# A list scheduler's durations for matmuls and transposes, replaced in a 22,915-instruction kernel

## The chip, the cores and the metric

The kernel runs on one core of one Trainium2 chip. The metric is device time in microseconds (us) of one execution, the median of the runs taken.

## The reference

Two transformer blocks in a row on 256 tokens of width 1024, float32 throughout, each followed by a norm:

```
memn = rmsnorm(mem)
layer 0: x += ab_mixer(rmsnorm(x));  x += cross_attn(rmsnorm(x), memn);  x += relu(h @ w1)^2 @ w2
layer 1: x += c_mixer(rmsnorm(x));   x += cross_attn(rmsnorm(x), memn);  x += relu(h @ w1)^2 @ w2
second block, layer 0: h += pool_mixer(rms_norm(h));     h += conv_glu_ffn(rms_norm(h))
second block, layer 1: h += window_attn(rms_norm(h));    h += conv_glu_ffn(rms_norm(h))
out = rms_norm(h)
```

`ab_mixer` is half a gated linear attention, half stick-breaking attention; `c_mixer` is a gated delta rule (short convolutions, a triangular inverse for each of 8 heads, then a chain of products for each head). The window attention has 16 heads. The weights are 1 MB blocks of float32, each used once.

## The kernel before, in words

**Arithmetic.** A float32 matrix is split on the chip into a high part (`hi`, ScalarE, line 402, a cast to the type float32r) and the rest (`lo`, VectorE, line 406). `mm3` (line 521) then issues three float32r matmuls, hi x hi, hi x lo, lo x hi, into one PSUM bank. This is nearly all the work: matmuls with 256 moving columns (`lin_b`, line 576) or with 512 (`second`, line 657, which adds a stage's result to the residual `xs`). Plain float32 matmuls, which appear as two instructions each, do the small products of the mixers; transposes (`tr`) are matmuls against an identity (`base` in the trace).

**Staging.** Each weight block goes by DMA to one of 2 `raw` buffers, is split into one of 3 `hi` and 3 `lo` buffers, and is consumed by 24 or 48 matmuls. The 8 PSUM banks (`pb`), 9 scratch tiles, 10 large tiles and 4 hidden pairs are slots that operations compete for.

**The order of instructions.** Nothing runs as it is written. Each helper calls `plan.add(engine, cost, ...)`, which records an operation, its operands and an estimated duration. At the end `Plan.run` (line 203) plays the engines against each other: an engine that is free takes, among the operations whose operands are complete and whose tiles find a slot, the one that comes first in the program. Between engines it adds a latency from a table (`LAT`, line 137). The order so found is emitted as a fixed instruction stream for each engine; on the chip an instruction waits by semaphore for its operands, and all that is behind it on its engine waits too. So a cost in `add` changes no instruction, only the order of them. Every kind of operation has its cost formula: ScalarE, VectorE, GpSimd (0.3 us plus a hundredth of a us for each element), DMA (361 GB/s and 2.5 us), and TensorE in `mm` (line 440) and `tr` (line 445).

Three other rules of `run` use these costs. Within 3.41 us windows of planned time it sums TensorE's cost, weighted by the share of rows used; after a window with less than 1.31 it doubles the cost of a TensorE operation (line 330). A ScalarE or VectorE operation over 0.25 us is held back when an operation marked urgent, earlier in the program, comes due within twice its duration (lines 292 to 298); urgent are the chains of the last two heads of `c_mixer` and the scaling before the pool mixer. SP issues a DMA only when the planned transfers reach less than 1 us ahead, and not more than 300 operations ahead of the first unfinished one, except for `raw` blocks.

**Places that matter below.** `finish` (line 1321) ends two heads of `c_mixer`: a power on GpSimd (`rs`), a scaling on VectorE (`vn`), then transposes. `head` (line 1537) is one pair of window-attention heads: scores, row maxima, exponentials, a division (`sw`, `prs`), three transposes each, products. `pool_mix` (line 1428) is the pool mixer. `Norm` (line 607) follows each `second`: sum into `xs`, four transposes, split into `hth`, `htl`.

Of the kernel before, what the change touches and what calls it, by code (L numbers as in the profile page):

```python
# [9 lines left out]
F32 = mybir.dt.float32  # L10
# [8 lines left out]
T = 256  # L19
# [108 lines left out]


class Plan:  # L130
    """Records the operations in program order, then issues them in the order of a list schedule.

    Every operation has an estimated cost. The schedule runs the engines against each other: an engine
    takes, of the operations whose operands are complete and whose tiles find a free slot, the one that
    comes first in the program. Program order alone defines what is computed."""

    LAT = {("PE", "PE"): 0.0, ("ACT", "ACT"): 0.06, ("DVE", "DVE"): 0.06, ("SP", "SP"): 0.0, ("ACT", "DVE"): 0.15,
           ("ACT", "PE"): 0.27, ("DVE", "ACT"): 0.13, ("DVE", "PE"): 0.21, ("PE", "ACT"): 0.2, ("PE", "DVE"): 0.2,
# [32 lines left out]
    def add(self, eng, cost, outs, ins, emit, late=0.0, table=None, whole=False):  # L171
        o = Op()
        o.eng, o.cost, o.late, o.emit, o.table = eng, cost, late, emit, table
        o.done, o.start = False, None
        o.urgent = self.urgent
        o.eager = any(ap.tensor.name.startswith("raw") for ap in outs)
        o.rows = ins[0].shape[0] / 128.0 if ins and eng == "PE" else 0.0
        o.at = len(self.ops)
        o.prio = o.at + self.shift
        o.succ, o.ready, o.tiles = [], 0.0, {}  # L180
        deps = {}
        for w, aps in ((False, ins), (True, outs)):
            for ap in aps:
                name, lo, hi, p0, p1 = self.span(ap)
                h = self.hist.setdefault(name, [])
                if name in self.home:
                    o.tiles[name] = True
                if w and whole:
                    lo, hi, p0, p1 = 0, 1 << 60, 0, 1 << 60
                for a, b, c, e, x, xw in h:  # L190
                    if (w or xw) and x is not o and a < hi and lo < b and c < p1 and p0 < e:
                        deps[id(x)] = x
                if w:
                    h[:] = [r for r in h if not (lo <= r[0] and r[1] <= hi and p0 <= r[2] and r[3] <= p1)]
                h.append((lo, hi, p0, p1, o, w))
        for n in o.tiles:
            self.left[n] += 1
        o.wait = len(deps)
        for x in deps.values():
            x.succ.append(o)  # L200
        self.ops.append(o)

    def run(self, tc):
        free = dict(self.size)
# [5 lines left out]
                span[n] = span.get(n, (o.at,))[0], o.at  # L210

        def safe(tag, y):
            """Whether the rest still finds its slots in program order once tile y has taken one."""
            ends = [span[n][1] for n in kinds[tag] if n in live and self.left[n]] + [span[y][1]]
            far = max(ends)
            todo = [n for n in kinds[tag] if n not in live and n != y]
            if not todo or span[y][0] <= span[todo[0]][0]:
                return len(ends) <= self.size[tag]
            for n in todo:
                a, b = span[n]  # L220
                if a > far:
                    break
                ends = [e for e in ends if e >= a] + [b]
                if len(ends) > self.size[tag]:
                    return False
            return True
# [12 lines left out]
        first = 0  # L239
# [12 lines left out]
        order = []  # L252
        now = 0.0
        while ev:
            now = ev[0][0]
            while ev and ev[0][0] <= now + 1e-9:
                _, kind, _, x = heapq.heappop(ev)
# [17 lines left out]
            if self.ops[first].done:  # L275
                while first < len(self.ops) - 1 and self.ops[first].done:
                    first += 1
                x = self.ops[first]
# [4 lines left out]
            for eng, h in heaps.items():  # L283
                if busy[eng] > now + 1e-9:
                    continue
                while h:
# [4 lines left out]
                    o = h[0][2]  # L291
                    if eng in soon and o.cost > 0.25:
# [3 lines left out]
                        if t:  # L296
# [3 lines left out]
                    new = [n for n in o.tiles if n not in live]  # L300
                    short = next((self.home[n] for n in new if free[self.home[n]] <= (self.keep[n] if o.at > first else 0)
                                  or not safe(self.home[n], n)), None)
                    if o.table and o.table != table:
                        a = wants.get(table, [])
# [16 lines left out]
                    cost = o.cost  # L321
# [6 lines left out]
                    if eng == "PE":  # L328
                        w = int(now * 3 / 10.24)
# [32 lines left out]
def tile_net(ctx: ExitStack, tc: tile.TileContext, d, out):  # L362
    nc = tc.nc
# [8 lines left out]
    one = ctx.enter_context(tc.tile_pool(name="one", bufs=1))  # L372
# [4 lines left out]
    add = plan.add  # L377

    def size(ap):
        n = 1  # L380
        for e in ap.shape[1:]:
            n *= e
        return n
# [7 lines left out]
    def act(out, in_, func, scale=1.0, bias=0.0, accum_out=None):  # L391
        kw = {}
        if accum_out is not None:
            kw["accum_out"] = accum_out
        if not (isinstance(bias, float) and bias == 0.0):
            kw["bias"] = bias
        if not (isinstance(scale, float) and scale == 1.0):
            kw["scale"] = scale
        table = {AF.Exp: "exp", AF.Ln: "exp", AF.Silu: "silu"}.get(func)
        add("ACT", 0.093 + size(out) / 1200.0 + (0.07 if aps_of(scale) else 0.0)  # L400
            + (0.107 if aps_of(accum_out) else 0.0), aps_of(out, accum_out),
            aps_of(in_, scale, bias), lambda: nc.scalar.activation(out=out, in_=in_, func=func, **kw), table=table)  # L402

    def tt(out, in0, in1, op, eng=None):
        add("DVE" if eng is None else "POOL", dve(size(out)) if eng is None else 0.3 + size(out) / 100.0, [out],
            [in0, in1], lambda: (eng or nc.vector).tensor_tensor(out=out, in0=in0, in1=in1, op=op))  # L406
# [25 lines left out]
    def memset(out, value, eng):  # L432
        add("DVE" if eng is nc.vector else "POOL", dve(size(out)), [out], [], lambda: eng.memset(out, value))
# [4 lines left out]
            lambda: (eng or nc.sync).dma_start(out=out, in_=in_), late=2.5 if eng is None else 4.0)  # L438

    def mm(o, lhsT, rhs, start, stop):  # L440
        n = 32 if size(lhsT) == 32 else max(size(rhs), 64)
        add("PE", n * (4 if rhs.dtype == F32 else 1) / 2400.0 + 0.0025, [o], [lhsT, rhs],
            lambda: nc.tensor.matmul(o, lhsT=lhsT, rhs=rhs, start=start, stop=stop), whole=start)  # L443

    def tr(o, i, idn=None):
        idn = ident if idn is None else idn
        add("PE", 0.056, [o], [i, idn], lambda: nc.tensor.transpose(o, i, idn))  # L447

    def pb(keep=0):
        return plan.tile("p", 8, psum.tile([128, 512], F32, tag="p", name="pb"), keep)  # L450

    def t512(*shape, dt=F32, name="t5"):
        return plan.tile("t", N_TMP, tmp.tile([128, *shape], dt, tag="t512", name=name))
# [35 lines left out]
    def split(hi, lo, src, scale=None):  # L489
        if scale is None:  # L490
            act(out=hi, in_=src, func=AF.Copy)
            tt(out=lo, in0=src, in1=hi.bitcast(F32), op=ALU.subtract)
        else:
            act(out=hi, in_=src, func=AF.Copy, scale=scale)
            stt(out=lo, in0=src, scalar=scale, in1=hi.bitcast(F32), op0=ALU.mult, op1=ALU.subtract)
# [25 lines left out]
    def mm3(o, ah, al, bh, bl, start, stop):  # L521
        mm(o, lhsT=ah, rhs=bh, start=start, stop=False)
        mm(o, lhsT=ah, rhs=bl, start=False, stop=False)
        mm(o, lhsT=al, rhs=bh, start=False, stop=stop)
# [16 lines left out]
    LO = 32  # L541
    sel = const.tile([64, 16], F32, name="sel")
    selr = const.tile([64, 16], F32R, name="selr")

    def lin_small(h, w, n):
        """The rows of w^T x for a few columns: the high parts of w give rows 0.., the low parts rows LO..,
        and sel adds the two."""
        wt = t512(8, 64, dt=F32R, name="wsm")
        memset(wt[:, :, 0:LO].bitcast(F32), 0.0, nc.gpsimd)
        split(wt[:, :, 0:n], wt[:, :, LO:LO + n], w)  # L550
        p = pb()
        for k in range(8):
            for q in range(2):
                mm(p[:LO + n, 0:T], lhsT=wt[:, k, :LO + n], rhs=h[q][:, k, :], start=k + q == 0, stop=k + q == 8)
        return p
# [7 lines left out]
        copy(dst.rearrange("p c n -> p (c n)"), gp[:, 0:2 * n])  # L563

    def stacked(src, n):
        """High and low parts of n rows, for row_bc."""
        s = t512(T, dt=F32R, name="stk")[:LO + n]
        memset(s[:LO].bitcast(F32), 0.0, nc.gpsimd)
        act(out=s[:n], in_=src, func=AF.Copy)
        tt(out=s[LO:], in0=src, in1=s[:n].bitcast(F32), op=ALU.subtract)  # L570
        return s
# [795 lines left out]
        return second(4, lambda g: hx[g], "c_out", nxt)  # L1367

    class Last:
        """The norm between the two blocks; with pool, also the pool mixer's own norm of its result:  # L1370
        ((x g r)^2 mean + eps)^-1/2 r = ((x g)^2 mean + eps (x^2 mean + eps))^-1/2 for each token."""
        halves = ((0, 0), (0, 1), (1, 0), (1, 1))

        def __init__(self, name, pool):
# [261 lines left out]
```

## Time and profile before

| | |
|---|---|
| median of 3 runs | 1361.91 us (1361.0 to 1365.15) |
| span of the profiled execution | 1359.9 us (its own device time is not listed) |
| instructions | 22,915 |
| TensorE matmuls, busy | 9,283 instructions, 1346.0 us (99%) |
| TensorE weight loads, busy | 1229.3 us (90%) |
| VectorE, ScalarE, GpSimd, busy | 953.0, 768.6, 65.9 us |
| mean granted TensorE clock | 0.999 of full speed |

The stages, in us from the start of the span, as they can be told by the tiles' names: ab mixer to 168, cross attention to 234, first MLP to 420, c mixer to 638, cross attention to 697, second MLP to 876, pool mixer to 891, first gated feed-forward to 1081, window attention to 1167, second gated feed-forward to 1347, last norm and output.

TensorE's busy time must be read with care. Matmuls are pipelined and a matmul's end is modelled: 256 columns are listed with a duration of 284 ns but start every 120 ns. An idle time in the table is therefore what is left after the modelled end; a delay of under about 0.16 us shows only in the start times.

### The profile page before, as it was taken

Reading aid. Unit: us, or ns where it says so; the run is one execution under the profiler, and the core shown is the slowest. Engines: PE = TensorE matmul, PEld = TensorE weight load, DVE = VectorE, ACT = ScalarE, POOL = GpSimd, SP = SyncE. Lnnn points to the kernel's source line nnn. Section 1 sums busy time; section 2 is a strip of 40 time slices with the busy share of each in tenths; the row PEclk is TensorE's granted clock in tenths of the full one; section 3 lists DMA queues with packets and bytes.
Section 4 is the critical chain, followed back from the end, with each engine's and each line's share of the span. In section 5 each row is a group of like instructions: output and inputs, shape, how many; then the busy total and the mean of one; then the engine's idle time right before and its main releaser. Section 6 shows DMA issues by size and latency. Waiting matters only on the chain.

```text
span 1359.9 us, 22915 instructions
## 1 busy us (share of the span) xinstructions
PE 1346.0 (99%) x9283; PEld 1229.3 (90%) x9283; DVE 953.0 (70%) x1668; ACT 768.6 (57%) x1368; POOL 65.9 (5%) x84
## 2 busy tenths in 40 slices
PE   9999999999999999999999999999999999999997
PEld 7889898999998998888999999899999997999997
DVE  5786566555558886677765555897777887877776
ACT  5584555444446755557664444675555666655554
POOL 1000000000000331111000000000000000000000
PEclk9999999999999999999999999999999999999999
DMA  7755453655552564344445556345555344455551
GB/s 289 252 190 187 155 194 108 216 190 191 191 189 102 191 225 141 140 177 143 147 161 198 190 190 251 126 169 203 187 186 190 126 154 140 155 206 187 186 188 72
DMA packets 41098, 240.65 MB, mean 177 GB/s; under 512 B 4608, under 2 KB 8992, under 8 KB 13856
## 3 DMA queue, kind: packets, MB, share of 16 engines
q1 hardware_dynamic: 38976, 233.53, 48.7%
q0 software_dynamic: 2016, 5.65, 1.4%
q8 instruction: 73, 1.20, 0.3%
q14 instruction: 33, 0.27, 0.1%
HBM read 232.60 MB, written 6.56 MB: 176 GB/s over the span
## 4 chain that ended last, share of the span: by engine, by line
PE 95%; DVE 2%; issue 1%; ACT 1%; DMA 0%; POOL 0%; SPq 0%; POOLq 0%; DVEq 0%
PE pb L443 93%; PE pb L447 2%; DVE lo L406 1%; DMA xt<-xT_dram 0%; POOL rs L406 0%; DVE xs L406 0%; DVE prs L410 0%; SPq L438 0%; DVE sw L430 0%; DVE htl L410 0%; ACT prs L402 0%; ACT hi L402 0%; DVE vn L410 0%; DVE pl L406 0%; ACT v1t L402 0%
## 5 line engine op out<-in xcount | busy, mean ns | idle before, releaser
L406 DVE TENSOR_TENSOR lo<-raw,hi 128x1024 fp32r<-128x1024 f32 (+1 forms) x422 | 504.1, 1210 | 221.8 <-ACT hi L402 220.8
L402 ACT ACTIVATE hi<-raw 128x1024 fp32r<-128x1024 f32 (+1 forms) x422 | 430.6, 1045 | 339.5 <-PE pb L443 294.2
L443 PE MATMUL pb<-hth,hi 128*128 128x256 f32 x1712 | 485.1, 285 | 2.1 <-ACT hi L402 1.6
L443 PE MATMUL pb<-htl,hi 128*128 128x256 f32 x1712 | 486.1, 284 | 0.0
L443 PE MATMUL pb<-hth,lo 128*128 128x256 f32 x1712 | 485.1, 284 | 0.1
L443 PEld LDWEIGHTS pb<-hth,hi 128*128 128x128 f32 x1712 | 327.2, 192 | 6.3 <-ACT hi L402 2.7
L443 PEld LDWEIGHTS pb<-htl,hi 128*128 128x128 f32 x1712 | 328.0, 192 | 3.1 <-issue 0.3
L443 PEld LDWEIGHTS pb<-hth,lo 128*128 128x128 f32 x1712 | 327.6, 192 | 1.5 <-DVE lo L406 1.0
L443 PE MATMUL pb<-lo,hh 128*128 128x512 f32 x592 | 233.1, 394 | 0.0
L443 PE MATMUL pb<-hi,hh 128*128 128x512 f32 x592 | 232.6, 393 | 0.0
L443 PE MATMUL pb<-hi,hl 128*128 128x512 f32 x592 | 231.4, 393 | 0.0
L443 PEld LDWEIGHTS pb<-hi,hl 128*128 128x128 f32 x592 | 111.2, 188 | 22.7 <-issue 0.2
L443 PEld LDWEIGHTS pb<-hi,hh 128*128 128x128 f32 x592 | 111.5, 188 | 21.0
L443 PEld LDWEIGHTS pb<-lo,hh 128*128 128x128 f32 x592 | 111.5, 188 | 20.3 <-issue 0.2
L410 DVE SCALAR_TENSOR_TENSOR f<-fu,prm,f 128x255 f32<-128x255 f32 (+1 forms) x176 | 74.0, 478 | 2.4 <-ACT f L402 2.4
L406 POOL TENSOR_TENSOR rstd<-s,pw 128x1 f32<-128x1 f32 (+1 forms) x22 | 21.0, 958 | 1051.0 <-DVE s L416 502.6
L406 DVE TENSOR_TENSOR fu<-pb,rbc 128x512 f32<-128x512 f32 (+1 forms) x48 | 30.8, 646 | 44.0 <-PE pb L443 43.7
L402 ACT ACTIVATE f<-fu,prm 128x256 f32<-128x256 f32 x88 | 47.8, 589 | 13.7 <-DVE fu L406 13.6
L402 ACT ACTIVATE junk<-xs 128x512 bf16<-128x512 f32 x44 | 27.9, 638 | 26.2 <-DVE xs L406 22.4
L410 DVE SCALAR_TENSOR_TENSOR htl<-pb,prm,hth 128x128 fp32r<-128x128 f32 x128 | 35.6, 343 | 5.7 <-ACT hth L402 5.7
L402 ACT ACTIVATE hth<-pb,prm 128x128 fp32r<-128x128 f32 x128 | 36.4, 375 | 4.9 <-PE pb L447 3.9
L443 PE MATMUL pb<-mh,hi 128*128 128x256 f32 x128 | 37.1, 290 | 0.0
(334 smaller groups left out, 1555.5 us busy)
## 6 DMA issues: line engine op xcount, KB each, us to landing
raw<-w_dram SPq DMA_DIRECT2D x64, 1024.0 KB, 4.8
raw<-fi_dram SPq DMA_DIRECT2D x44, 1024.0 KB, 4.8
raw<-fo_dram SPq DMA_DIRECT2D x22, 1024.0 KB, 4.9
raw<-kv_dram SPq DMA_DIRECT2D x16, 1024.0 KB, 4.9
raw<-c_in_dram SPq DMA_DIRECT2D x16, 1024.0 KB, 4.9
raw<-ab_in_dram SPq DMA_DIRECT2D x10, 1024.0 KB, 5.3
raw<-q_dram SPq DMA_DIRECT2D x8, 1024.0 KB, 4.9
raw<-o_dram SPq DMA_DIRECT2D x8, 1024.0 KB, 4.8
```

The lines of the kernel that those rows point to most:

```text
L402: aps_of(in_, scale, bias), lambda: nc.scalar.activation(out=out, in_=in_, func=func, **kw), table=table)
L406: [in0, in1], lambda: (eng or nc.vector).tensor_tensor(out=out, in0=in0, in1=in1, op=op))
L410: lambda: nc.vector.scalar_tensor_tensor(out=out, in0=in0, scalar=scalar, in1=in1, op0=op0, op1=op1))
L443: lambda: nc.tensor.matmul(o, lhsT=lhsT, rhs=rhs, start=start, stop=stop), whole=start)
L447: add("PE", 0.056, [o], [i, idn], lambda: nc.tensor.transpose(o, i, idn))
```

## The change

Two cost formulas are replaced: that of a matmul and that of a transpose. Docstrings are also left out (blank lines keep the line numbers up to `mm`; behind it they move by 6).

```
     def mm(o, lhsT, rhs, start, stop):
-        n = 32 if size(lhsT) == 32 else max(size(rhs), 64)
-        add("PE", n * (4 if rhs.dtype == F32 else 1) / 2400.0 + 0.0025, [o], [lhsT, rhs],
+        n = size(rhs)
+        if size(lhsT) == 32:
+            cost = 0.056
+        elif rhs.dtype == F32:
+            cost = 2 * max(n / 1200.0 + 0.004, 0.106)
+        else:
+            cost = max(n / 2400.0 + 0.0133, 0.108)
+        add("PE", cost, [o], [lhsT, rhs],
             lambda: nc.tensor.matmul(o, lhsT=lhsT, rhs=rhs, start=start, stop=stop), whole=start)
 
     def tr(o, i, idn=None):
         idn = ident if idn is None else idn
-        add("PE", 0.056, [o], [i, idn], lambda: nc.tensor.transpose(o, i, idn))
+        add("PE", 0.1, [o], [i, idn], lambda: nc.tensor.transpose(o, i, idn))
```

| operation | planned before, us | planned after, us |
|---|---|---|
| float32r, 512 columns | 0.2158 | 0.2266 |
| float32r, 256 columns | 0.1092 | 0.1200 |
| float32, 256 columns | 0.4292 | 0.4347 |
| float32, 128 columns | 0.2158 | 0.2213 |
| float32, 64 columns or fewer | 0.1092 | 0.2147 or 0.2120 |
| float32, 32 x 32 blocks | 0.0558 | 0.0560 |
| transpose | 0.0560 | 0.1000 |

## Rows read from the trace of the kernel before

**Rows 1.** The page: busy time, share of the span and instructions of each engine.
```profile
PE 1346.0 (99%) x9283; PEld 1229.3 (90%) x9283; DVE 953.0 (70%) x1668; ACT 768.6 (57%) x1368; POOL 65.9 (5%) x84
```

**Rows 2.** Busy time by stretch; columns as in the first line.
```profile
core 0: us, PE busy (x) PEld busy (x) DVE busy (x) ACT busy (x) POOL busy (x), PEclk, DMA share, GB/s
0.00:34.00 34.00, 30.91 (x220) 26.75 (x221) 18.78 (x38) 19.86 (x39) 4.80 (x14) 1.00 0.79 289
...
234.00:420.00 186.00, 186.00 (x1209) 170.29 (x1209) 104.05 (x123) 90.14 (x123) 2.60 (x3) 1.00 0.53 188
...
510.00:638.00 128.00, 127.08 (x999) 109.44 (x999) 86.39 (x200) 74.58 (x197) 12.74 (x17) 1.00 0.41 145
...
876.00:891.00 15.00, 13.24 (x109) 12.40 (x108) 14.10 (x36) 11.21 (x34) 1.09 (x2) 1.00 0.28 104
...
1081.00:1167.00 86.00, 84.90 (x614) 73.48 (x613) 68.20 (x189) 58.75 (x151) 1.07 (x2) 1.00 0.37 129
...
1347.00:1360.00 13.00, 5.86 (x26) 4.50 (x24) 6.88 (x16) 4.19 (x10) 1.10 (x2) 0.88 0.22 81
```

**Rows 3.** Chain that ended last, in order of time: start, us, what.
```profile
234.10 179.62 PE pb L443 x1168
```

**Rows 4.** Timeline, first MLP: start, us, engine, line, operation, tiles, shape, count.
```profile
399.82 0.39 PE L443 MATMUL pb<-hi,hl 128*128 128x512 f32 x1
...
400.50 0.39 PE L443 MATMUL pb<-hi,hl 128*128 128x512 f32 x1
...
401.08 0.28 PE L443 MATMUL pb<-hth,hi 128*128 128x256 f32 x1
...
403.96 0.28 PE L443 MATMUL pb<-hth,hi 128*128 128x256 f32 x1
```

**Rows 5.** Chain that ended last: four transposes in the norm before the last feed-forward.
```profile
1157.52 0.44 PE pb L447 x4
```

**Rows 6.** Timeline of TensorE at the pool mixer: float32, 128 columns.
```profile
875.01 2.84 PE L443 MATMUL pb<-pool_a,xg 128*128 128x128 f32 x24
877.60 0.36 PE L443 MATMUL pb<-hi,ph 128*128 128x256 f32 x1
```

**Rows 7.** TensorE's waits: engine, line, released by: total us, times, longest.
```profile
PE pb L443 <- ACT hi L402: 1.6, 2, 1.0
PE pb L469 <- POOL pw L433: 1.3, 1, 1.3
PE pb L447 <- DVE prs L416: 1.1, 2, 0.7
PE pb L447 <- DVE vn L410: 0.9, 4, 0.4
PE pb L443 <- DVE pl L406: 0.5, 1, 0.5
PE pb L443 <- ACT hth L402: 0.5, 1, 0.5
PE pb L443 <- DVE pool_a L416: 0.5, 1, 0.5
PE pb L447 <- DVE s L416: 0.3, 1, 0.3
```

**Rows 8.** Timeline of TensorE in the c mixer, where small blocks alternate with full ones.
```profile
514.30 0.49 PE L443 MATMUL pb<-hi,htl 128*128 128x512 f32 x1
514.75 0.23 PE L443 MATMUL pb<-x,ti 32*32 32x32 f32 x2
514.90 0.38 PE L443 MATMUL pb<-mh,hi 128*128 128x256 f32 x1
515.22 0.22 PE L443 MATMUL pb<-x,ti 32*32 32x32 f32 x2
...
611.43 0.49 PE L443 MATMUL pb<-hi,hh 128*128 128x512 f32 x1
611.85 0.33 PE L443 MATMUL pb<-ti,x 64*64 64x64 f32 x2
```

**Rows 9.** Chain that ended last, at the end of one pair of heads in the c mixer.
```profile
531.17 0.15 DVE rs L406
...
532.42 1.05 POOL rs L406
...
533.70 0.36 DVE vn L410
...
534.10 0.33 PE pb L447
```

**Rows 10.** Chain that ended last, first pair of heads of the window attention.
```profile
1100.77 0.56 DVE prs L410
...
1108.02 1.14 DVE lo L406
...
1109.47 0.36 DVE prs L416
...
1109.97 0.41 PE pb L447 x2
```

## Prediction

> **What bounds the kernel now.** I read the page's busy times first. TensorE is busy for 1346.0 of 1359.9 us, and the next engine, VectorE, for 953.0 [rows 1]. The reader should conclude one thing: the time is TensorE's own work, and an order of instructions can only give back what TensorE waits. The table by stretch says where it waits: 3.09 us in the first 34 us (34.00 - 30.91), 7.14 us in the last 13, 0.92 in the c mixer, 1.76 at the pool mixer, 1.10 in the window attention, and nothing in the stretch of the first MLP [rows 2]. The granted clock is 1.00 in all of these but the last, where the matmuls run out [rows 2]; no order can win clock.
>
> The ends of matmuls are modelled, so I went on to start times. In the first MLP three matmuls of 512 columns take 400.50 - 399.82 = 0.68 us, 0.227 each, and 24 of 256 columns 403.96 - 401.08 = 2.88 us, 0.120 each [rows 4]. That stage has 16 blocks of 48 matmuls of 256 columns and 16 of 24 of 512: 768 x 0.120 + 384 x 0.227 = 92.2 + 87.2 = 179.4 us. The chain of waits has there one piece of 179.62 us with 1168 matmuls, these 1152 and a few more, and no other engine in it [rows 3]. So the bulk stages hold no slack at all, and the chain confirms it: it never leaves TensorE in them. The chain leaves TensorE only where heads or norms end: 531.17 to 534.10 [rows 9], 1100.77 to 1109.97 [rows 10].
>
> **What can be moved.** Idle that an order can touch: 0.92 + 1.76 + 1.10 = 3.78 us [rows 2]. The list of waits agrees: of its 6.7 us, 1.3 belong to the warm-up matmuls and 1.6 to the first blocks from DMA (ACT `hi`), which leaves 3.8 [rows 7]. Start and tail don't move with TensorE's costs: the first waits for DMA, the tail follows the last matmul.
>
> Some delay hides under the modelled ends. A 256-column matmul before a 32 x 32 block holds TensorE for 515.22 - 514.90 = 0.32 us instead of 0.12, and no idle is listed; in [rows 8] stand the first two and the last of 12 such places in the c mixer, each with 0.15 to 0.22 us over the pitch, 2.3 us together. They are part waits, part the cost of changing the block's size, and no formula of the change prices the latter. So what a better order can reach is between 3.8 us and 3.8 + 2.3 = 6.1 us, 0.45% of the span. That is the ceiling of the gain, unless shorter delays, which I did not count, go as well.
>
> **The change, part by part.** It adds and removes no instruction, transfer or wait: 9,283 matmuls run at the same pitch. Its parts can only act through the order.
>
> (1) float32r matmuls, 0.0108 us dearer each. The old formula gave the first MLP 768 x 0.1092 + 384 x 0.2158 = 166.7 us, the new one gives 768 x 0.1200 + 384 x 0.2266 = 179.2, against 179.6 in the trace [rows 3]. So the plan's clock ran 7% fast for TensorE and now runs right. In the bulk stages I cost that at 0: splits and transfers (VectorE 104.05 and ScalarE 90.14 of 186 us) run ahead by whole blocks of 5.8 us (48 x 0.12), which is the cover. If that cover went, each block would show a wait of up to a split, 1.14 us [rows 10]; a slower planned TensorE makes the others run further ahead, not less.
>
> (2) Transposes from 0.056 to 0.1, measured 0.44 / 4 = 0.11 [rows 5]. In the ten norms these 16 transposes become 0.7 us longer in the plan. They lie between matmuls that are ready, so 0 as well.
>
> (3) Plain float32: 24 instructions of 128 columns take 877.60 - 875.01 = 2.59 us, 0.216 for each pair [rows 6]; planned 0.2158 before and 0.2213 now, no matter. With 64 columns or fewer the plan's cost doubles, 0.109 to 0.212; these are the triangular inverses and row sums of the c mixer. There the plan believed TensorE done with small products too early, so it interleaved the eight heads on a false clock. Here I expect a gain, since a chain's next step is then slotted where its operand really arrives. Bounds: nothing, or all of that stage's waits, 0.92 listed + 2.3 hidden = 3.2 us. I take 1.0, nearer to nothing, because the places in [rows 8] are mostly changes of block size.
>
> (4) The cushion goes. This is the part that speaks against the change. When a chain leaves TensorE, the plan fills the planned latency with other matmuls. Those ran 10% longer on the chip than planned (0.120 for 0.109), and that surplus covered latencies planned too short. One such is plain: the power on GpSimd is planned at 0.3 + 4 / 100 = 0.34 us and takes 1.05 [rows 9], 0.71 short, and its four `finish` waits already show 0.9 us together [rows 7]. From `rs` at 531.17 to the transposes at 534.10 are 2.93 us; 9% of it, 0.26 us, times four is 1.1 us more waiting. For the eight pairs of window heads (two wait today, 1.1 us [rows 7]) the latency from scores to transposes is 1109.97 - 1100.77 = 9.2 us [rows 10]; its cushion of 0.8 us may or may not be what keeps the other six from waiting. Bounds 0 and 8 x 0.8 = 6.4 us; I take 0.4, half of one head, because VectorE, not a latency, fills that stretch.
>
> (5) The doubling after a sparse window and the DMA pacing. Dearer matmuls reach the 1.31 more easily, so fewer are doubled, and the granted clock of 1.00 [rows 2] says none should be. No row shows which were. Bounds: -1.0, the longest wait for `hi` goes, to +1.0, another like it comes [rows 7]; I take 0, since the first blocks are paced by their transfers.
>
> Sum: -1.0 + 1.1 + 0.4 = +0.5 us on a span of 1359.9 us. The median of the runs shown, 1361.9, is 2.0 above that span; the span's own run is not listed, and the lowest run is 1361.0. I forecast 1361.9 + 0.5, rounded down to 1362 since the shorter delays count on that side, no change.
>
> **A rule against it.** The trace's 256-column pitch is 0.12 us [rows 4]. The Trainium skill, "TensorE: Matmul & The Clock Gate", section "Back-to-back issue gap", gives the warm gap as N / 2.4 + 2.5 ns, an estimate of 109 ns here: the old formula to the digit. By that rule the new costs would be 10% too dear and the first MLP would be done in 166.7 us. Its 179.6 us say otherwise [rows 3], so for these float32r matmuls the trace decides. The same skill, "Trainium Kernel Development and Optimization", section "Best Practices", says to judge distance from the roofline by the busy share of the weight loads rather than of the matmuls. That reads 90% here, an estimate of 130 us of room. In the dense first MLP it is 170.29 / 186 = 92% with no slack in the chain [rows 2, 3], so the missing tenth is no room.
>
> **The rivals.** A: the clean-up works. The c mixer, pool mixer and window attention lose most of the 6.1 us, about 5 us, 1357. For it: all three stages are where the old costs were wrong by the most. Against: the waits for `prs`, `vn`, `pl` and `pool_a`, 1.1 + 0.9 + 0.5 + 0.5 = 3.0 of the 3.8 us, are released by VectorE [rows 7], whose costs stay as they are. 0.27.
>
> B: slower. The lost cushion is the mechanism; its place is the window attention and the c mixer's `finish`. Price: 1.1 us + 6.4 us, less the 1.0 of (3), so +6.5, 1368. It decides once five of the eight window pairs wait 0.8 us longer (1.1 - 1.0 + 5 x 0.8 = 4.1). For it: the GpSimd power is planned at a third of its time. Against: six of the eight pairs show no wait today. 0.23.
>
> C: the order hardly changes, because TensorE always has a ready matmul and takes the first in the program. Then 1361.9, inside my forecast.
>
> **How the numbers follow.** My forecast with C has 0.50. I call 0.3% (4.1 us) the least that can be told from no change here; the three runs themselves differ by that. Faster needs two thirds of the 6.1 us, which is A, 0.27; slower is B, 0.23. The likeliest case's own range is 1358 to 1366. The range takes in all but the far end of A and most of B: 1355.5 to 1367.5.
>
> **What would show it.** Right: a piece of some 179.6 us in the first MLP and granted clock 1.00, `vn` waits of 0.9 us or a little more, fewer delays before small blocks, and the sum of waits within 3 us of 6.7. Wrong: new waits of TensorE in a bulk stage, which would mean that part (1) is not free; `prs` waits above 4 us (B); or the idle of 510 to 638, 876 to 891 and 1081 to 1167 nearly gone (A).

## The result, and the profile after

The changed kernel takes 1382.8 us (median of 4 runs, 1380.95 to 1385.0), the kernel before 1361.45 beside it: a ratio of 1.0152, interval 1.0138 to 1.0166. It is slower by 21 us, where I had forecast no change.

The page of the changed kernel, busy time as in [rows 1]. Its span is 1380.3 us.
```profile
PE 1350.5 (98%) x9283; PEld 1228.9 (89%) x9283; DVE 954.5 (69%) x1668; ACT 767.6 (56%) x1368; POOL 68.1 (5%) x84
```

The span grew by 20.4 us (1380.3 - 1359.9) and TensorE's busy time by 4.5. So 15.9 of the 20.4 are idle: the instructions are the same, and TensorE waits more. Its waits, in the columns of [rows 7] (L449 is now `mm`, L453 `tr`):
```profile
PE pb L449 <- ACT pool_a L402: 3.6, 1, 3.6
PE pb L453 <- DVE prs L416: 3.2, 4, 1.5
PE pb L449 <- ACT hi L402: 2.8, 2, 1.4
PE pb L453 <- DVE s L416: 2.2, 1, 2.2
PE pb L453 <- DVE vn L410: 2.0, 4, 0.7
PE pb L453 <- DVE bkh L419: 1.9, 1, 1.9
PE pb L453 <- ACT vt L402: 1.7, 3, 0.7
PE pb L475 <- POOL pw L433: 1.3, 1, 1.3
PE pb L449 <- ACT kT L402: 1.1, 1, 1.1
PE pb L449 <- DVE dg L416: 0.8, 3, 0.4
PE pb L449 <- DMA ti<-d_t: 0.8, 1, 0.8
```
These eleven come to 21.4 us; the whole list of before came to 6.7 [rows 7]. No wait became enormous. There are simply more of them, on chains of every kind: the pool mixer's scaling (`pool_a`), the window heads (`prs`), the norms (`s`, `dg`), the c mixer's heads (`vn`, `bkh`, `vt`, `kT`).

The bulk kept its pace. The chain that ended last, in the first MLP; the piece that answers to [rows 3]:
```profile
235.42 179.93 PE pb L449 x1170
```

The table by stretch of the changed kernel, columns in the first line, for the first part of the c mixer, the stages of [rows 2] and three short pieces of the pool mixer:
```profile
core 0: us, PE busy (x) PEld busy (x) DVE busy (x) ACT busy (x) POOL busy (x), PEclk, DMA share, GB/s
...
421.00:512.00 91.00, 86.44 (x640) 80.17 (x638) 75.27 (x172) 56.08 (x110) 24.76 (x26) 1.00 0.48 164
512.00:645.00 133.00, 129.38 (x1018) 110.69 (x1016) 88.52 (x202) 76.14 (x200) 18.52 (x23) 1.00 0.42 149
...
885.00:908.90 23.90, 17.53 (x116) 16.25 (x115) 18.47 (x41) 14.98 (x40) 2.73 (x3) 0.86 0.39 146
...
1099.00:1189.00 90.00, 86.32 (x630) 75.08 (x629) 70.93 (x194) 59.49 (x159) 2.48 (x3) 1.00 0.34 123
...
888.00:892.00 4.00, 0.62 (x3) 0.42 (x3) 3.37 (x8) 2.48 (x5) 1.62 (x1) 0.95 0.30 94
892.00:894.00 2.00, 1.80 (x8) 1.80 (x9) 2.00 (x3) 0.15 (x1) 0.00 (x0) 0.50 0.84 344
896.00:898.00 2.00, 2.00 (x11) 2.00 (x11) 0.85 (x2) 1.04 (x3) 0.00 (x0) 0.50 0.94 385
```
The first part of the c mixer in the kernel before:
```profile
420.00:510.00 90.00, 90.00 (x666) 84.75 (x664) 78.17 (x177) 58.94 (x113) 27.17 (x33) 1.00 0.55 181
```
Idle is 4.56 us in the first part of the c mixer (nothing before), 3.62 in its second part (0.92), 6.37 at the pool mixer (1.76) and 3.68 in the window attention (1.10). That is 14.5 of the 15.9 us. At the pool mixer the granted clock falls to 0.50, TensorE's lower level (1.2 of 2.4 GHz), right after a stretch in which TensorE did 0.62 us of work in 4 us; before it stayed at 1.00 there.

**Where the 20.4 us lie, stage by stage.** A mark that both kernels have is the first transposition in each stage's closing norm. The table gives how many us longer each stretch between two marks took than before, in the profiled executions of this kernel and of the main experiments below. In the kernel before the marks stand at 158.27, 223.96, 413.56, 629.37, 687.33, 885.77, 1075.29, 1157.36 and the end of the span.

| stretch that ends in the closing norm of | after | e1 | e2 | e3 | e4 | e15 | e16 | e17 | e12 |
|---|---|---|---|---|---|---|---|---|---|
| ab mixer | -0.1 | 0.7 | 0.5 | -1.8 | -1.0 | -1.1 | 2.4 | -0.8 | -0.9 |
| cross attention 1 | 1.4 | 1.1 | 0.0 | 1.5 | 0.2 | 0.0 | 1.2 | 0.0 | 0.2 |
| MLP 1 | 0.3 | 0.2 | 0.1 | 0.4 | 0.2 | 0.4 | 0.4 | -0.1 | 0.2 |
| c mixer | 5.6 | 5.4 | 1.5 | -5.5 | -1.6 | 3.7 | 7.4 | 5.8 | -2.7 |
| cross attention 2 | 1.9 | 0.9 | 1.2 | 2.6 | 0.6 | -0.3 | 2.0 | 0.0 | -1.4 |
| pool mixer (with MLP 2) | 5.6 | 6.3 | -0.2 | 5.0 | 5.8 | 0.4 | 3.2 | 5.1 | 0.4 |
| feed-forward 1 (from the pool mixer's end) | 3.1 | 0.0 | 3.0 | 0.7 | 0.4 | 3.2 | 0.5 | 1.4 | 3.1 |
| window attention | 1.6 | 2.5 | -0.6 | 1.7 | 0.9 | 0.0 | 2.6 | 1.2 | 0.6 |
| feed-forward 2 and the end | 1.1 | 1.0 | -0.1 | 0.6 | 0.1 | 0.1 | 1.2 | 0.0 | 0.1 |

MLP 1, pure bulk, loses 0.3 us. The c mixer, MLP 2's closing norm with the pool mixer, and the stretch behind it lose 14.3 of the 20.4.

**The dearest place read closely.** ScalarE's timeline at the pool mixer, first after, then before; columns as in [rows 4], in brackets the idle time ahead and what ended it.
```profile
886.62 0.63 ACT L402 ACTIVATE junk<-xs 128x512 bf16<-128x512 f32 x1
...
887.51 1.05 ACT L402 ACTIVATE hi<-raw 128x1024 fp32r<-128x1024 f32 x1
888.46 0.62 ACT L402 ACTIVATE junk<-xg 128x512 bf16<-128x512 f32 x1
889.08 1.04 ACT L402 ACTIVATE hi<-raw 128x1024 fp32r<-128x1024 f32 x1
891.64 0.51 ACT L402 ACTIVATE pool_a<-pool_a,rstd 128x256 f32<-128x256 f32 x1 [1.52 <-POOL rstd L406]
```
```profile
876.82 0.62 ACT L402 ACTIVATE junk<-xs 128x512 bf16<-128x512 f32 x1
...
877.43 0.62 ACT L402 ACTIVATE junk<-xg 128x512 bf16<-128x512 f32 x1
...
879.35 0.51 ACT L402 ACTIVATE pool_a<-pool_a,rstd 128x256 f32<-128x256 f32 x1 [0.93 <-POOL rstd L406]
```
The chain is: two sums of squares (`junk`), the power on GpSimd (`rstd`), the scaling `pool_a`, on which TensorE's next ready work hangs. Before, the second square follows the first at once, and `pool_a` starts 2.53 us after the first square; after, a weight split (`hi`, 1.05 us) stands between the squares, and it takes 5.02 us. GpSimd's timeline (last section) shows the power of 889.99 itself at 1.62 us, where before it took 0.70 at 878.61. So the 2.49 us have three parts: the second square starts 1.23 us later behind the first, the power 0.35 later behind the second square, and the rest, 0.91, is the power's own length. TensorE's timeline shows what follows:
```profile
892.20 5.49 PE L449 MATMUL pb<-pool_a,xg 128*128 128x128 f32 x24 [3.58 <-ACT pool_a L402]
897.34 0.56 PE L449 MATMUL pb<-hi,ph 128*128 128x256 f32 x1
```
Start to start, the 24 instructions take 897.34 - 892.20 = 5.14 us, against 2.59 at full clock [rows 6]: 2.55 us more on top of the wait of 3.58. The granted clock is at 0.50 from 891.6 to 898.4; with the matmuls behind the 24 the half clock costs 3.1 us, half of TensorE's 6.2 us of work in that time.

### The profile page after: what moved, and what is told of

It is laid out like the page before. It is cut to its first block, busy times and chain, and to the rows that moved or that the text cites. A ratio compares the mean times of both kernels' runs of the same rounds, so it can differ in the third digit from the quotient of the medians.

```text
span 1380.3 us, 22917 instructions
## 1 busy us (share of the span) xinstructions
PE 1350.5 (98%) x9283; PEld 1228.9 (89%) x9283; DVE 954.5 (69%) x1668; ACT 767.6 (56%) x1368; POOL 68.1 (5%) x84
## 4 chain that ended last, share of the span: by engine, by line
PE 84%; DVE 6%; issue 4%; ACT 3%; POOL 2%; DMA 1%; SPq 0%; POOLq 0%; ACTq 0%; DVEq 0%
PE pb L449 82%; DVE lo L406 2%; PE pb L453 2%; ACT hi L402 1%; ACT prs L402 1%; DVE prs L410 1%; POOL rstd L406 1%; DMA xt<-xT_dram 0%; DVE sw L430 0%; POOL rnk L406 0%; DVE htl L410 0%; POOL rs L406 0%; POOL ti L438 0%; POOL rnq L406 0%; DVE vt L410 0%
## 5 line engine op out<-in xcount | busy, mean ns | idle before, releaser
L449 PE MATMUL pb<-hth,hi 128*128 128x256 f32 x1712 | 484.6, 284 | 2.9 <-ACT hi L402 2.8
L449 PE MATMUL pb<-htl,hi 128*128 128x256 f32 x1712 | 485.7, 284 | 0.0
L449 PE MATMUL pb<-hth,lo 128*128 128x256 f32 x1712 | 484.4, 284 | 0.0
L449 PEld LDWEIGHTS pb<-hth,hi 128*128 128x128 f32 x1712 | 327.3, 192 | 6.7 <-ACT hi L402 3.5
L449 PEld LDWEIGHTS pb<-htl,hi 128*128 128x128 f32 x1712 | 328.0, 192 | 2.6
L449 PEld LDWEIGHTS pb<-hth,lo 128*128 128x128 f32 x1712 | 327.8, 192 | 0.6 <-DVE lo L406 0.4
L449 PE MATMUL pb<-lo,hh 128*128 128x512 f32 x592 | 233.0, 394 | 0.0
L449 PE MATMUL pb<-hi,hh 128*128 128x512 f32 x592 | 232.3, 393 | 0.0
L449 PE MATMUL pb<-hi,hl 128*128 128x512 f32 x592 | 231.9, 393 | 0.0
L449 PEld LDWEIGHTS pb<-hi,hl 128*128 128x128 f32 x592 | 111.3, 188 | 23.2 <-DVE hl L406 0.6
L449 PEld LDWEIGHTS pb<-hi,hh 128*128 128x128 f32 x592 | 111.4, 188 | 21.0 <-ACT hh L402 0.4
L449 PEld LDWEIGHTS pb<-lo,hh 128*128 128x128 f32 x592 | 111.5, 188 | 20.4 <-issue 0.2
L449 PE MATMUL pb<-hi,htl 128*128 128x512 f32 (+1 forms) x96 | 36.9, 384 | 0.0
L449 PE MATMUL pb<-mh,hi 128*128 128x256 f32 x128 | 36.8, 288 | 0.0
```

## The experiments

**The theories.** T1, the cushion: with float32r planned 10% short, each chain that leaves TensorE had more real TensorE work behind it than the plan believed. That covered latencies planned too short elsewhere, the GpSimd power above all. T2, the small products: the new costs of plain float32 and transposes did it. T3, luck: any other order is some 20 us worse than one that happens to be good. Each ratio is to runs of the kernel before on the same chip, whose medians were 1361.1 to 1361.6.

**Which half: e1_r_only, e2_small_only.** e1 is the kernel before with the new float32r line alone; e2 is the changed kernel with the old one back:
```
# e1, on the kernel before
-        add("PE", n * (4 if rhs.dtype == F32 else 1) / 2400.0 + 0.0025, ...
+        cost = n * 4 / 2400.0 + 0.0025 if rhs.dtype == F32 else max(n / 2400.0 + 0.0133, 0.108)
+        add("PE", cost, ...
# e2, on the changed kernel
-            cost = max(n / 2400.0 + 0.0133, 0.108)
+            cost = max(n, 64) / 2400.0 + 0.0025
```


> The new duration for float32r matmuls alone (0.120 and 0.2266 us for 256 and 512 columns); plain float32 and transposes planned as before. Cushion theory (planned matmuls that were 10% short made the plan put more matmul time behind every chain than the plan's own clock showed, and that covered latencies planned too short): the fillers are all float32r, so most of the 21 us comes, 12 to 21 us slower than before, with the waits for VectorE and GpSimd results in the c mixer, the pool mixer and the window attention. Small-products theory (the doubled costs of transposes and of small float32 products turned the chains' order round): near the kernel before, within 4 us. Luck theory (the order before is one lucky draw of the list schedule, any other costs draw another): anywhere from 4 to 25 us slower.

> The other half alone: plain float32 with 64 columns or fewer 0.212 instead of 0.109, transposes 0.1 instead of 0.056; float32r as before. Cushion theory: within 5 us of before, for the fillers keep their short durations. Small-products theory: 15 to 21 us slower. Luck theory: 4 to 25 us slower, with no relation to the first run.

e1 took 1378.47 us (1.012, 1.0105 to 1.0136), e2 1366.83 (1.0034, 1.0022 to 1.0045): +16.9 and +5.3. The float32r durations carry four fifths of the loss, and T2 is worth the rest. In e1's profile only 5.4 us of a span longer by 17.9 are idle. From the start times of the 9,283 matmuls I worked out by how much each exceeds its own pitch. Before, 8 exceed it by over 0.5 us (5.9 us together) and 370 by 0.05 to 0.5 us (39.0). In the changed kernel it is 18 (22.2) and 412 (42.6), in e1 12 (11.9) and 461 (49.4). Some 3 us of the short excesses, in the changed kernel and in e1 alike, are the half clock at the pool mixer. Without them the changed kernel has about as many as before, and e1 some 7 us more. So the changed kernel loses by long waits and the half clock, and e1 to a good part by many short excesses, which the list of waits doesn't show. A short excess can be a wait or a change of the block's size [rows 8]; no run separates the two.

**More planned time for the other engines: e3_pool_cost, e4_lat.** Both are the changed kernel; e3 raises the planned cost of a GpSimd elementwise operation, e4 adds 0.1 us to each latency between engines.
```
# e3
-        0.3 + size(out) / 100.0 ...      (GpSimd tensor_tensor)
+        1.2 ...
# e4
+    LAT = {k: v + (0.1 if k[0] != k[1] else 0.0) for k, v in LAT.items()}
-                        lat = self.LAT.get((x.eng, y.eng), 0.1)
+                        lat = self.LAT.get((x.eng, y.eng), 0.2)
```


> The kernel after, and GpSimd's two-operand operation (the power in every norm and head) planned at 1.2 us, near what the traces show (0.55 to 2.6 us), instead of 0.3 us and a hundredth of a us for each element. Cushion theory: the chain with the largest underestimate is planned right, so a third to a half of the loss returns, 7 to 11 us less than after, most of it at the pool mixer (3.6 us wait for pool_a and the half clock behind it) and at the norms that wait for dg. Luck theory: a change of either sign against after, no place singled out.

> The kernel after, and 0.1 us more for every latency between two engines in the plan's table. Cushion theory: a cushion is given back by another way, at each hop of a chain, so half or more of the loss returns, 10 to 20 us less than after. Luck theory: no systematic gain, within 8 us of after on either side. Small-products theory: no gain, the small products are still dear.

e3: 1366.94 us (1.0038, 1.0023 to 1.0053); e4: 1367.86 (1.0043, 1.0028 to 1.0058). Either one, alone, gives back some 15 of the 21 us with the matmul durations left as measured. TensorE's largest waits, e3, then e4:
```profile
PE pb L453 <- DVE prs L416: 3.7, 4, 1.5
PE pb L449 <- DVE pool_a L416: 3.4, 1, 3.4
```
```profile
PE pb L450 <- ACT pool_a L403: 3.6, 1, 3.6
```
e3 returns more than the 7 to 11 us that I expected, and at another place: most of it in the c mixer (5.6 down to -5.5). The pool mixer still waits 3.4 us. There the power takes 1.61 us in e3 too, more than the 1.2 now planned, and ScalarE again runs a split between the two squares. So a higher power cost alone did not settle the pool mixer.

**The same on the kernel before: e8_before_pool.** The edit of e3 on the kernel before.


> The kernel before with GpSimd's two-operand operation planned at 1.2 us, its matmul durations untouched. Cushion theory: the waits for vn and the pool mixer's scaling that still show before shrink, 0 to 5 us faster. Luck theory: 4 to 20 us slower.

1361.9 us (1.0007, 0.9994 to 1.002). No gain, where I had expected 0 to 5 us. Its four `vn` waits (0.9 us in [rows 7]) are gone from the list and the time is the same. That fits T1, if under the old durations the cushion already paid for the short power cost; but T1 had led me to expect a small gain, and I read the result so only afterwards.

**Ratio, not matmuls: e15_scaled, e16_scaled_down.** e15 is the changed kernel with every other duration and latency times 1.08; e16 is the kernel before with them times 0.926 and its matmul durations untouched.
```
+        if eng != "PE":
+            cost, late = cost * K, late * K          # K = 1.08 (e15), 0.926 (e16)
+    LAT = {k: v * K for k, v in LAT.items()}         # and the default, table load and issue times
```


> The kernel after with every planned duration and latency of the other engines and of the transfers times 1.08, so that TensorE's share of the plan is as before (its float32r durations rose by 5 to 10%) while its own durations stay the measured ones. If what counts is TensorE's planned time against the other engines' (cushion theory), nearly all of the float32r loss of 17 us returns: 1361 to 1369. If small products and transposes or luck decide: 1375 to 1390.

> The reverse: the kernel before, its matmul durations untouched, every planned duration and latency of the others times 0.926. Cushion theory: the loss of the change is had without touching a matmul's duration: 1370 to 1385, with waits for vn, prs, pool_a. If the matmuls' own durations mattered for their own sake: within 5 us of before.

e15: 1368.81 us (1.0051, 1.0036 to 1.0066), 14 us given back. e16: 1382.37 (1.0151, 1.0134 to 1.0168). e16 touches no matmul's or transposition's duration, and it loses as much as the changed kernel. TensorE's largest waits in e16, and that for `pool_a`:
```profile
PE pb L450 <- DVE vn L413: 2.6, 4, 1.0
PE pb L446 <- ACT hi L405: 2.5, 2, 1.4
PE pb L450 <- DVE prs L419: 2.5, 3, 1.3
PE pb L446 <- DVE pl L409: 1.5, 2, 1.2
PE pb L446 <- ACT kT L405: 1.4, 1, 1.4
...
PE pb L446 <- DVE pool_a L419: 0.2, 1, 0.2
```
Four chains come late as in the changed kernel (`vn`, `hi`, `prs`, `kT`). `pool_a`, which I had named as well, does not: it waits 0.2 us, not 3.6. In its place `pl` is late, the ab mixer loses 2.4 us, and the clock is at 0.50 from 584.8 to 588.2, in the c mixer. So the size of the loss is the same, and its places are so only in part. What matters is TensorE's planned time relative to that of the other engines. This is the strongest evidence for T1.

**How much, and in both directions: e5_nudge, e6_half, e7_short.** The kernel before with another float32r and float32 formula; its own is `/ 2400.0 + 0.0025`.
```
e5:  / 2400.0 + 0.0035        e6:  / 2400.0 + 0.0079        e7:  / 2520.0 + 0.0
```


> The kernel before with 0.001 us more for each matmul instruction planned (a tenth of the change's 0.0108 for float32r), transposes as before. It measures how much the schedule moves by mere disturbance. Cushion theory: a tenth of the cushion is gone, 0 to 4 us slower than before. Luck theory: a new draw, 4 to 20 us slower like any other.

> The kernel before with the constant at 0.0079 instead of 0.0025: half of the change for float32r, transposes as before. The run with 0.001 more was 1.8 us slower than before, that with the full float32r change 16.9. Cushion theory: between these, 4 to 14 us slower, with waits in the same places. Luck theory: a draw like any other, 0 to 20 us slower; a time near before or beyond the full change would speak for it.

> The kernel before with matmuls planned shorter still: columns / 2520 without a constant (0.1016 for 256 and 0.2032 for 512 columns, 15% and 10% under the measured 0.120 and 0.227). The cushion is larger by half. Cushion theory: no loss, within 4 us of before on either side. Luck theory: 4 to 20 us slower.

e5 1362.94 us (1.0009, 1.0 to 1.0019), e6 1365.35 (1.0025, 1.0014 to 1.0037), e7 1371.51 (1.0074, 1.0054 to 1.0094). With e1, which changes float32r alone: 0.001 us a matmul costs 1.8, 0.0054 costs 3.7, 0.0108 costs 16.9. The jump from e6 to e1 lies mostly at the pool mixer (0.1 and 6.3 us over before) and in the c mixer (2.2 and 5.4). The price grows with the dose, though not in proportion, and a small nudge, which any theory of luck would let cost as much as a large one, costs little. That speaks against T3 in its plain form. But e7 missed: still shorter durations, a bigger cushion, lose 10.4, inside the range that I had given T3. Its waits are others:
```profile
PE pb L443 <- DVE htl L410: 1.7, 2, 1.4
PE pb L443 <- DVE lo L406: 1.4, 2, 0.8
PE pb L443 <- DMA ti<-d_t: 1.4, 1, 1.4
```
In the norm before the window attention 12 of e7's 16 transposes stand in one batch (1084.25 to 1085.58), and TensorE then waits for the split of their result (`htl`). My expectation had taken the cushion as one-sided. Of the formulas tried on the kernel before its own is the best; why e7 loses 6.6 us in the c mixer I did not find.

**Where the durations act: e17_bulk_only.** A flag gives the new durations only to what the two MLPs and the two feed-forwards record, their closing norms included, and the old ones elsewhere.


> The new durations for the operations of the two MLPs and the two gated feed-forwards with their closing norms, the old ones everywhere else. These four stages hold 5,000 of the 9,283 instructions, but no chains except at their ends. Cushion theory: 0 to 6 us slower, at the norms that close them; the rest of the loss needs the mixers. Luck theory: 4 to 25 us slower, at any place.

1374.06 us (1.009, 1.0075 to 1.0105), +12.7: a miss, I had expected little. It lies outside the range of T1 and inside that of T3. TensorE's two largest waits:
```profile
PE pb L452 <- ACT pool_a L403: 3.6, 1, 3.6
PE pb L452 <- DMA ti<-d_t: 2.4, 1, 2.4
```
The matmuls of the bulk lose nothing here either (MLP 1: -0.1). But what borders on the bulk does: at MLP 2's end a split again stands between the pool mixer's squares (+5.1). And the c mixer loses 5.8, as much as in the changed kernel, although its own costs are the old ones, and by other waits: the chain there runs over a DMA (`ti<-d_t`) that became late, and from 580.6 to 584.0 the clock is at 0.50. So part of the loss, here the 5.8, is not the price of a local cushion, but of how a stage happens to meet the next. Of T3 that much stays.

**The pool mixer alone: e14_urgent_only, e11_urgent.** The squares and means of MLP 2's closing norm are marked urgent, so that a split is held back when one of them is about to come due; in e14 on the changed kernel, in e11 with the power at 1.2 as well.
```
+            plan.urgent = self.pool
             act(out=j, in_=xs[:, i, s], func=AF.Square, ...)
...
                 ts(ss[:, 0:1], ss[:, 0:1], EPS, ALU.add)
+                plan.urgent = False
```


> The kernel after with one thing changed: the sum, squares and means ahead of the pool mixer are marked urgent (durations all as after). Cushion theory, with the split between the two squares as the cause at this place: the 3.6 us wait for pool_a and the half clock behind it (24 instructions in 5.1 instead of 2.6 us) go, 5 to 8 us less than after, 1374 to 1378; the rest of the loss stays in the other stages. Luck theory: no change that is tied to this place; after plus or minus 8 us.

> The kernel after with GpSimd planned at 1.2 us and, at the norm ahead of the pool mixer, the sum, squares and means marked urgent, so that no split of 1 us is put between the two squares. In the third experiment TensorE still waited 3.4 us for pool_a there and ran at half its clock for some 5 us behind it. Cushion theory, with the split as the piece of the chain that is short of cover at this place: that wait falls under 2 us, the clock stays at full, 4 to 7 us less than the third experiment, about 1360 to 1363. Luck theory: a change of either sign, spread over all stages.

e14: 1376.64 us (1.0115, 1.0094 to 1.0135), 6 less than the changed kernel. e11: 1364.98 (1.0022, 1.0013 to 1.0031), 2 less than e3 and short of what I expected: `pl` is late by 1.8 there too. e14's two rows of the pool mixer among TensorE's waits, then its table for the stretch 888 to 892:
```profile
PE pb L449 <- DVE pl L406: 1.8, 1, 1.8
PE pb L449 <- ACT pool_a L402: 0.4, 1, 0.4
```
```profile
888.00:892.00 4.00, 2.44 (x14) 2.24 (x14) 3.57 (x9) 2.76 (x6) 1.35 (x1) 0.83 0.02 4
```
The two squares now follow each other (885.76 and 886.55), and `pool_a` starts 3.63 us after the first, in place of 5.02; the power still takes 1.61. TensorE's waits there are 1.8 + 0.4 = 2.2 us in place of 3.6, so the split between the squares was one part of the cause, and the power's length remains. The clock still falls (0.83 here): the full clock that I had expected of e14 did not come. In the profiled executions e14 saves 4.5 us, 1.5 of them in the pool mixer's stretch and 2.8 in the one behind it, where the wait of 2.2 us for `s` is gone.

**Both repairs: e9_pool_lat, e12_urgent_lat, e18_best.** e9 is e3 and e4 together; e12 adds the urgent squares; e18 is e12 with a float32r constant of 0.0079 in place of 0.0133, half of the change.


> The kernel after with both corrections: GpSimd at 1.2 us and 0.1 us more for every latency between engines. Cushion theory: both repair the same shortage, so the gains overlap; 1360 to 1367, with the wait for pool_a of about 3.5 us still there, since neither run with one of them removed it. Luck theory: 1361 to 1385.

> All three: GpSimd at 1.2 us, 0.1 us more for each latency, urgent squares ahead of the pool mixer. Cushion theory: the wait for pool_a goes as well; 1355 to 1362, at or under the kernel before. Luck theory: 1361 to 1385.

> A try for a version that beats both: GpSimd at 1.2 us, 0.1 us more for each latency, urgent squares, and the float32r constant at 0.0079 instead of 0.0133. If cushion and corrected latencies add up without overshooting, 1354 to 1360. If too much cover costs as much as too little (the run with still shorter matmuls lost 10 us), 1361 to 1370.

e9 1366.17 us (1.0032, 1.0021 to 1.0043): the two repairs don't add up. Each alone had already brought the c mixer under its old time (table), and the wait for `pool_a` stays at 3.6. e12 1362.97 (1.0007, 0.9998 to 1.0016): all repairs together return the changed kernel to the time of before, just above the range that I gave. e18 1360.42 (0.9993, 0.9983 to 1.0002): the fastest median of all, between the two ranges that I gave, and no measurable gain. No version that I ran is faster than the kernel before by more than its interval. But e5, e8, e12 and e18 are four other orders within 1.8 us of it, so it isn't true that any other order is some 20 us worse, as T3 has it.

## Why the prediction was wrong

**The step that failed is (4), the lost cushion.** Its direction was right, and rival B was named for it. Its price was not: I took 1.1 + 0.4 us, with 7.5 as the far bound. The float32r line alone, where the cushion lies, costs 16.9 us (e1), and shrinking the other engines' planned time instead costs 21.0 (e16). B's place was right only in part: the window attention lost 1.6 us, and `prs` waits 3.2 us, under the 4 that I had set as B's sign. Three things made step (4) small on paper.
- I priced it at two places, `finish` and the window heads. It was paid at other chains as well. `vn` went from 0.9 to 2.0 us and `prs` from 1.1 to 3.2, in all +3.2 where I had +1.5: the two places that I priced were not far off. But `bkh`, `vt`, `kT`, `dg` and `s`, absent or at 0.3 in [rows 7], now wait 7.7 us together.
- The pool mixer had no price at all. A 0.5 us wait there became 3.6 and pulled 3.1 us of half clock behind it. I had the short plan of the power in hand and applied it only to `finish`.
- I took an excess of 9% of a chain's length as the loss. A plan that believes in more slack also puts other work ahead of the chain: a whole split of 1.05 us between two squares. There the loss came in units of what is slotted in, not in per cent; for the other places that is not shown.

**Step (1), bulk at 0:** right inside it, 179.93 us against 179.62 [rows 3], MLP 1 +0.3. Wrong at its ends (e17: +5.1 at MLP 2's closing norm). The formula that the prediction quotes from the Trainium skill ("TensorE: Matmul & The Clock Gate", section "Back-to-back issue gap") is given there for a single, isolated matmul; that the first MLP would take 166.7 us by it was my use of it.

**Steps (2) and (3), transposes and small products:** the sign was wrong. I took -1.0; e2, which has just these, is +5.3. That their places are mostly block changes [rows 8] was a reason to expect no gain, and I still counted one. Two slips change nothing in this: the trace has eight norms with 16 such transposes, not ten, and the new formula gives 0.2120 for every plain float32 matmul of 64 columns or fewer, so the 0.2147 in the table of the change belongs to none.

**Step (5), doubling and DMA:** not tried alone. The waits for `hi` went from 1.6 to 2.8 us, 1.2 where my bound was 1.0; the ab mixer's stretch, in which they lie, took 0.1 us less all the same.

**"No order can win clock"** was half the truth: an order can lose it (0.50 from 891.6 to 898.4, where before it stayed at 1.00).

**The ceiling.** The argument from 3.8 to 6.1 us of movable idle bounded the gain, and the gain was bounded so: e18 found none. I then let the same number set the scale of the loss. Idle that is small because an order fits well says nothing of how much a misfit costs. Rival A failed, and the list of waits fits the reason that I gave against it: they hang on engines whose costs stayed as they were.

**What stays open.** Of the 21 us some 15 come back by any of three ways of giving the other engines more planned time (e3, e4, e15). The rest, about 5, is of the size of what e17 shows carried from stage to stage, and I can't assign it. That the ratio of the planned times matters is shown (e1, e15, e16). That each chain lost a cushion of its own is only argued: e17's c mixer loses as much without it, and the stretch behind the pool mixer loses some 3 us in the changed kernel, e2, e15 and e12 alike. A kernel whose costs had been chosen by trial would also lose on both sides, as with e7; no run here tells that apart from T1. Which operation of the c mixer costs which part is not settled either.

## What to carry to other kernels

In this list scheduler the costs of the engines work as ratios. Correcting one engine's costs alone can take away what its error was covering in the others: look at the worst under-estimate off that engine first (here the GpSimd power, planned 0.34 us, taking 1.05 and more), or correct all together. Here that only brought the time of before back (e12). And a small idle time bounds what a new order can win, never what it can lose.

## What the runs showed of the hardware

The GpSimd power on 128 x 2 elements, in MLP 2's closing norm, once for each half of the tokens; GpSimd's timeline of the kernel before, then of the changed one, then one row of VectorE's timeline of the changed one:
```profile
869.75 0.88 POOL L406 TENSOR_TENSOR rstd<-s,pw 128x2 f32<-128x2 f32 x1 [169.06 <-DVE s L410]
878.61 0.70 POOL L406 TENSOR_TENSOR rstd<-s,pw 128x2 f32<-128x2 f32 x1 [7.99 <-DVE s L410]
```
```profile
879.49 1.62 POOL L406 TENSOR_TENSOR rstd<-s,pw 128x2 f32<-128x2 f32 x1 [170.49 <-DVE s L410]
889.99 1.62 POOL L406 TENSOR_TENSOR rstd<-s,pw 128x2 f32<-128x2 f32 x1 [8.88 <-DVE s L410]
```
```profile
889.83 1.22 DVE L406 TENSOR_TENSOR lo<-raw,hi 128x1024 fp32r<-128x1024 f32 x1
```
The same instruction took about twice as long, and over the first 1.06 us of the last one VectorE ran a split. The kept traces of all 18 kernels bear it out: they hold 396 such powers in the norms, of 128 x 1 or 128 x 2 elements. Each of the 146 that took more than 1.2 us (1.40 to 2.80) ran beside a weight split on VectorE (`lo<-raw,hi`) for at least 0.97 us; the other 250 (0.54 to 1.14) did so for at most 0.65 us, most of them not at all. So the power's length depends on the order, and one planned cost can't fit it. That the split is the cause is still an inference; no run varied it alone.

TensorE's granted clock was 0.50 from 891.6 to 898.4, beginning in the wait of 3.58 us at the pool mixer, which ended at 892.20; behind the wait of 0.5 us for `pool_a` before [rows 7] it stayed at 1.00 [rows 2]. A long wait is not the only thing that it falls behind. In e17 it was 0.50 from 580.6 to 584.0 without any idle time listed before it: from 577.0 to 580.6 TensorE counts as busy throughout, with 23 instructions, blocks of 64 x 64 and matmuls of 256 columns in turn.
